# Gate and up projections of four SwiGLU layers by quadrants: seven block products in place of eight, with operand sums made on the chip

## The chip, the cores and the metric

The kernel runs on one core of a Trainium2 chip. TensorE (PE) multiplies, VectorE (DVE), ScalarE (ACT) and GpSimd (POOL) do elementwise work, and SyncE (SP) issues most DMAs. The metric is the device time of one execution in microseconds (us), the median of several runs.

## The reference, cut to what matters

A streaming encoder step over 560 columns (512 frames of a new stream, 32 of a running one, 16 meta tokens), two layers. Each layer is FFN, mixer, FFN: the first mixer is gated linear attention (GLA), the second multi-head latent attention (MLA). So there are four FFNs, called (1,0), (2,0), (1,1), (2,1): first or second FFN of layer 0 or 1. They run in this order: (1,0), GLA, (2,0), (1,1), MLA, (2,1). Each is

```python
def swiglu_half(h, norm_w, w_gate, w_up, w_down):   # h [560, 1024], D_FF = 2816
    hn = rmsnorm(h, norm_w)
    return h + 0.5 * ((jax.nn.silu(hn @ w_gate) * (hn @ w_up)) @ w_down)
```

All is float32.

## The kernel before, in words

Features lie on partitions, so `h` is 8 tiles of [128, 560]. The 560 columns are treated as two halves of 280 (272 in the last FFN, called hf 0 and hf 1), since a product goes to one PSUM bank.

Every operand of a matmul is split in two parts, `hi` (rounded to the fp32r type) and `lo` (the rest), and a product is three matmuls: hi·hi, lo·hi, hi·lo. `split` makes the parts with one ACT copy (L160, to `hi`) and one DVE subtraction (L161, to `lo`). A weight piece is [128, 1024] at most: a DMA to `raw` (2 buffers), then the split to `whi` and `wlo` (4 buffers each). `mm` (L188, L189, L191) sums over the tiles k of the contraction:

```python
for k, (xh, xl) in enumerate(xs):
    pe.matmul(out, hi[:, b0 + k, :], xh[:, c], start=k == 0, stop=False)      # L188
    pe.matmul(out, lo[:, b0 + k, :], xh[:, c], start=False, stop=False)       # L189
for k, (xh, xl) in enumerate(xs):
    pe.matmul(out, hi[:, b0 + k, :], xl[:, c], start=False, stop=k == n - 1)  # L191
```

`ffn` goes through the 22 tiles f of D_FF in three groups of 8, 7 and 7. For each f and each half it makes G (gate) and U (up), each with 24 matmuls over the 8 tiles of `h` (so 96 for one f). Then follow on DVE and ACT: `sg` = G times the norm's column scale `yn` (L279), Silu (ACT, L280), times the scale again (L281), `av` = U times `sg` (L283), and the split of `av` into `ah` and `al`. After a group its down projection runs: for 8 tiles m and two halves, 8 or 7 tiles of `ah`, `al`, three matmuls each, and DVE adds the result to `h` (L298). PSUM has 3 banks under the tag `ps` and 5 under `s`.

During the last group's down projection `after(m, hf)` is called for every updated piece of `h`: it makes the next stage's operand (`Normed.parts`: one ACT op L112, one DVE op L113) and the sum of squares for the norm (ACT L209, DVE L210). The norm's column scale is applied to results, so products needn't wait for it.

Tile's scheduler fixes at build time in which order each engine takes its instructions; the engines are in order and wait on semaphores. All pools of `ffn` are opened at its start and closed at its end. The start is written out by hand (`manual_schedule`): a first `h` piece of 280 KB, then the first weight in four pieces.

Of the kernel before, what the change touches and what calls it, by code (L numbers as in the profile page):

```python
# [18 lines left out]
P = 128  # L19
D = 1024  # L20
# [9 lines left out]
GROUPS = ((0, 8), (8, 15), (15, 22))  # L30
# [22 lines left out]
def weight_plan():  # L53
    """Offset and columns of every weight piece [128, columns]; plan lists (key, columns / 128) in the order of use."""
# [79 lines left out]

class Net:
    def __init__(self, ctx, tc, a):
        self.tc, self.nc, self.a, self.ctx = tc, tc.nc, a, ctx
        E = lambda **k: ctx.enter_context(tc.tile_pool(**k))
        self.g = E(name="g", bufs=1)
        self.w = E(name="w", bufs=4)  # L140
        self.xp = E(name="xp", bufs=20)
# [39 lines left out]
    def mm(self, out, w, b0, xs, cols):  # L181
        """out += sum over k of w[:, b0+k].T @ xs[k][:, cols], both operands in two parts."""
# [3 lines left out]
        pe = self.nc.tensor  # L186
        for k, (xh, xl) in enumerate(xs):
            pe.matmul(out, hi[:, b0 + k, :], xh[:, c], start=k == 0, stop=False)  # L188
            pe.matmul(out, lo[:, b0 + k, :], xh[:, c], start=False, stop=False)  # L189
        for k, (xh, xl) in enumerate(xs):  # L190
            pe.matmul(out, hi[:, b0 + k, :], xl[:, c], start=False, stop=k == n - 1)  # L191
# [20 lines left out]
    def rsqrt_mean(self, half, y, n, dim):  # L212
        """y[:, t] = 1 / sqrt(mean of squares of column t + eps), the same on every partition."""
# [41 lines left out]
    def ffn(self, i, l, xs, halves, after):  # L255
        nc = self.nc
        with self.tc.tile_pool(name=f"act{i}{l}", bufs=1) as ap, \
                self.tc.tile_pool(name=f"tmp{i}{l}", bufs=3) as tp:
            for gi, (f0, f1) in enumerate(GROUPS):
                acts = [(ap.tile([P, T], F32R, name=f"ah{j}", tag=f"ah{j}"),  # L260
                         ap.tile([P, T], F32R, name=f"al{j}", tag=f"al{j}")) for j in range(f1 - f0)]
                order = [(f, hf) for f in range(f0, f1) for hf in (0, 1)]
                if gi == 0:
                    order = [(f0, 0), (f0 + 1, 0), (f0, 1), (f0 + 1, 1)] + order[4:]
                L = {}
                for f, hf in order:
# [12 lines left out]
                    nc.vector.tensor_tensor(sg[:, :n], G[:, :n], y, op=ALU.mult)  # L279
                    nc.scalar.activation(sg[:, :n], sg[:, :n], AF.Silu)  # L280
                    nc.vector.tensor_tensor(sg[:, :n], sg[:, :n], y, op=ALU.mult)  # L281
                    av = tp.tile([P, 280], F32, name="av", tag="av")
                    nc.vector.tensor_tensor(av[:, :n], U[:, :n], sg[:, :n], op=ALU.mult)  # L283
                    self.split(acts[f - f0][0][:, c], acts[f - f0][1][:, c], av[:, :n])
                last = gi == len(GROUPS) - 1
                order = [(m, hf) for m in range(ND) for hf in (0, 1)]
                if last:
                    order = order[:8] + [(m, 0) for m in range(4, 8)] + [(m, 1) for m in range(4, 8)]
                L = {}
                for m, hf in order:  # L290
                    if m not in L:
                        L[m] = self.load(("d", i, l, gi, m))
                    c0, c1 = halves[hf]
                    n = c1 - c0
                    c = slice(c0, c1)
                    Y = self.bank()
                    self.mm(Y[:, :n], L[m], 0, acts, halves[hf])
                    nc.vector.scalar_tensor_tensor(self.h[:, m, c], Y[:, :n], 0.5, self.h[:, m, c],  # L298
                                                   op0=ALU.mult, op1=ALU.add)
# [23 lines left out]
    def gla(self, xs, after, one, con):  # L323
        nc, tc, a = self.nc, self.tc, self.a
        nv = self.nv
        mask, causal, causs, wgu, aTs, aTq, facs, onec = con
        bg, hn = NORM_COLS["bg"], NORM_COLS["hn"]
        with ExitStack() as es:
            E = lambda **k: es.enter_context(tc.tile_pool(**k))
            one = E(name="gl1b", bufs=1)  # L330
            two = E(name="gl2", bufs=2)
            op = E(name="glo", bufs=8)
# [3 lines left out]
            # the last 48 frames as one operand: the high parts in columns 0..47, the low parts in columns 64..111  # L336
# [26 lines left out]
            def values(h):  # L363
                """v of the head by frames; for the first head also the gate's low rank part."""
# [97 lines left out]
            for h in range(GH):  # L462
# [25 lines left out]
                # chunks: the group's 16 first frames, the running stream's frames, then pairs of 64  # L488
# [62 lines left out]
                # output gate, and the projections that fill the gaps of the chunks  # L551
# [43 lines left out]
            wout(1)  # L595

# [14 lines left out]
    def softmax(self, pool, p, parts):  # L611
        """p = softmax over the columns of all parts (tile, rows' column count, first column in p)."""
# [16 lines left out]
    def mla_constants(self, one):  # L629
# [12 lines left out]
        with self.tc.tile_pool(name="mlc", bufs=1) as tp:  # L642
# [15 lines left out]
    def mla(self, xs, after, one, kp, rp, ks, rs, kt, cq):  # L658
        nc, tc, a = self.nc, self.tc, self.a
        nv = self.nv  # L660
        (kph, kpl), (rph, rpl), (ksh, ksl), (rsh, rsl), (kth, ktl), (cqh, cql) = kp, rp, ks, rs, kt, cq
        with ExitStack() as es:
            E = lambda **k: es.enter_context(tc.tile_pool(**k))
            two = E(name="ml2", bufs=2)
            with tc.tile_pool(name="mlk", bufs=1) as kp:
# [79 lines left out]
                self.split(kth[:LS, 2, :], ktl[:LS, 2, :], tr[:LS, :256])  # L745
            cqs = [(cqh[:, m, :], cql[:, m, :]) for m in range(3)]
            self.attention(es, two, cqs, yq, [partial(f, 1) for f in (query_roots, query_norm)], kph, kpl, rph, rpl, ksh, ksl, rsh, rsl, kth, ktl, after)

    def attention(self, es, two, cqs, yq, query_norm, kph, kpl, rph, rpl, ksh, ksl, rsh, rsl, kth, ktl, after):
        nc, tc, a = self.nc, self.tc, self.a  # L750
        pe = nc.tensor
        E = lambda **k: es.enter_context(tc.tile_pool(**k))
        at = E(name="at", bufs=1)
# [41 lines left out]
        def sample(g):  # L795
            """The running stream's 32 frames of four heads, as 128 queries of the latent keys."""
# [19 lines left out]
            def latent2():  # L816
                """Every head's queries times the keys of all four; a head keeps its own."""
# [100 lines left out]
        def scores(h, t):  # L918
            """Softmax of the scores of 128 frames to pt[t]."""
# [54 lines left out]
        def wout(heads):  # L974
# [263 lines left out]
```

## Time and profile before

| what | us |
|---|---|
| median of 3 runs | 2156.37 (2156.29 to 2158.45) |
| span of the profiled execution | 2155.1 |
| PE busy | 2131.7 (16262 matmuls) |
| DVE busy | 1166.9 |
| ACT busy | 765.0 |
| POOL busy | 48.3 |

The profiled execution has no time of its own beside its span; the median lies 1.3 us above the span, which stands for what lies around it. Busy time counts overlapping matmuls once. The granted TensorE clock is 0.996 of full speed over the span.

### The profile page before, as it was taken

What the parts mean: (1) busy time and instruction counts of PE and PEld (TensorE: products, weight loads), DVE (VectorE), ACT (ScalarE), POOL (GpSimd) and SP (SyncE); (2) the same over time, 40 slices, a digit from 0 to 9 for tenths busy, and PEclk for the clock granted to TensorE, in tenths of its full rate; (3) what the DMA queues carried; (4) which work ended last, traced back from release to release, by engine and by line L of the source; (5) the groups of instructions that cost most, each with busy time, mean ns of one, the idle gap of its engine ahead of it and who ended that gap; (6) DMA issues with size and microseconds to landing.
All of it is one profiled execution on the core that took longest, in us unless ns stands there. A gap on an engine that the chain in (4) does not pass through costs nothing.

```text
span 2155.1 us, 38573 instructions
## 1 busy us (share of the span) xinstructions
PE 2131.7 (99%) x16262; PEld 2092.7 (97%) x16262; DVE 1166.9 (54%) x2487; ACT 765.0 (35%) x1463; POOL 48.3 (2%) x117
## 2 busy tenths in 40 slices
PE   8999999999999999999999999999999999999998
PEld 8999999989999999999999999999988899999997
DVE  7434444666657544434564344446787774344445
ACT  6212222455445322222342222224575553222231
POOL 0000000001110000000000000000110000000000
PEclk9999999999999999999999999999999999999999
DMA  5222222322222322232232222222111222222222
GB/s 164 84 89 85 83 89 74 90 68 76 65 81 74 98 87 81 84 93 79 88 91 89 88 79 89 87 86 85 57 58 42 88 79 88 89 86 84 96 78 72
DMA packets 57325, 180.17 MB, mean 84 GB/s; under 512 B 6384, under 2 KB 13936, under 8 KB 57152
## 3 DMA queue, kind: packets, MB, share of 16 engines
q1 hardware_dynamic: 53328, 173.07, 25.9%
q10 hardware_dynamic: 3824, 4.63, 0.7%
q8 instruction: 128, 2.10, 0.4%
q14 instruction: 45, 0.37, 0.1%
HBM read 173.69 MB, written 3.99 MB: 82 GB/s over the span
## 4 chain that ended last, share of the span: by engine, by line
PE 96%; DVE 2%; ACT 1%; DMA 1%; issue 0%; POOL 0%; SPq 0%; DVEq 0%; ACTq 0%; POOLq 0%
PE ps L188 21%; PE ps L191 20%; PE ps L189 20%; PE s L188 8%; PE s L191 8%; PE s L189 8%; PE ps L384 1%; PE ps L385 1%; PE ps L387 1%; PE ps L195 1%; PE s L195 1%; PE s L932 0%; PE s L948 0%; PE ps L196 0%; PE ps L197 0%
## 5 line engine op out<-in xcount | busy, mean ns | idle before, releaser
L160 ACT CAST whi<-raw 128x1024 fp32r<-128x1024 f32 (+4 forms) x351 | 342.9, 980 | 726.5 <-PE ps L191 555.8
L161 DVE TENSOR_TENSOR wlo<-raw,whi 128x1024 fp32r<-128x1024 f32 (+4 forms) x351 | 403.1, 1151 | 204.4 <-ACT whi L160 203.8
L188 PE MATMUL ps<-x,whi 128*128 128x280 f32 (+1 forms) x1872 | 497.4, 295 | 8.9 <-ACT whi L160 6.2
L189 PE MATMUL ps<-x,wlo 128*128 128x280 f32 (+1 forms) x1872 | 491.7, 292 | 0.0
L188 PE MATMUL s<-x,whi 128*128 128x280 f32 (+1 forms) x1424 | 371.3, 291 | 0.0
L189 PE MATMUL s<-x,wlo 128*128 128x280 f32 (+1 forms) x1424 | 370.4, 290 | 0.0
L188 PE MATMUL ps<-ah,whi 128*128 128x280 f32 (+1 forms) x1408 | 368.3, 290 | 0.0
L189 PE MATMUL ps<-ah,wlo 128*128 128x280 f32 (+1 forms) x1408 | 368.3, 291 | 0.0
L188 PEld LDWEIGHTS ps<-x,whi 128*128 128x128 f32 x1872 | 353.8, 189 | 13.6 <-ACT whi L160 6.2
L189 PEld LDWEIGHTS ps<-x,wlo 128*128 128x128 f32 x1872 | 353.9, 189 | 0.8 <-DVE wlo L161 0.2
L191 PE MATMUL ps<-x,whi 128*128 128x280 f32 (+1 forms) x1872 | 285.1, 291 | 0.0
L188 PEld LDWEIGHTS s<-x,whi 128*128 128x128 f32 x1424 | 268.2, 188 | 0.1
L189 PEld LDWEIGHTS s<-x,wlo 128*128 128x128 f32 x1424 | 267.7, 188 | 0.1
L188 PEld LDWEIGHTS ps<-ah,whi 128*128 128x128 f32 x1408 | 264.8, 188 | 0.0
L189 PEld LDWEIGHTS ps<-ah,wlo 128*128 128x128 f32 x1408 | 264.8, 188 | 0.0
L191 PEld LDWEIGHTS ps<-x,whi 128*128 128x128 f32 x1872 | 256.5, 189 | 0.5
L191 PE MATMUL ps<-al,whi 128*128 128x280 f32 (+1 forms) x1408 | 211.6, 291 | 0.0
L191 PE MATMUL s<-x,whi 128*128 128x280 f32 (+1 forms) x1424 | 211.2, 290 | 0.0
L298 DVE SCALAR_TENSOR_TENSOR h<-ps,h 128x280 f32<-128x280 f32 (+1 forms) x192 | 85.9, 447 | 227.2 <-PE ps L191 227.0
L191 PEld LDWEIGHTS s<-x,whi 128*128 128x128 f32 x1424 | 192.6, 188 | 0.0
L191 PEld LDWEIGHTS ps<-al,whi 128*128 128x128 f32 x1408 | 192.2, 188 | 0.0
L279 DVE TENSOR_TENSOR sg<-ps,yn 128x280 f32<-128x280 f32 (+1 forms) x176 | 78.0, 447 | 166.0 <-PE ps L191 165.6
(323 smaller groups left out, 2084.5 us busy)
## 6 DMA issues: line engine op xcount, KB each, us to landing
raw<-W SPq DMA_DIRECT2D x256, 512.0 KB, 3.5
raw<-W SPq DMA_DIRECT2D x64, 448.0 KB, 3.3
raw<-W SPq DMA_DIRECT2D x4, 384.0 KB, 3.1
h<-xT SPq DMA_DIRECT2D x2, 560.0 KB, 6.1
o_y<-h SPq DMA_DIRECT2D x8, 136.0 KB, 1.8
o_y<-h ACTq DMA_DIRECT2D x8, 136.0 KB, 1.8
raw<-W SPq DMA_DIRECT2D x8, 128.0 KB, 2.1
raw<-W SPq DMA_DIRECT2D x4, 256.0 KB, 2.7
```

Of the source, the lines that this page charges most:

```text
L160: self.nc.scalar.copy(hi, src)
L161: self.nc.vector.tensor_tensor(lo, src, hi.bitcast(F32), op=ALU.subtract)
L188: pe.matmul(out, hi[:, b0 + k, :], xh[:, c], start=k == 0, stop=False)
L189: pe.matmul(out, lo[:, b0 + k, :], xh[:, c], start=False, stop=False)
L191: pe.matmul(out, hi[:, b0 + k, :], xl[:, c], start=False, stop=k == n - 1)
L195: pe.matmul(out, a[0], b[0], start=first, stop=False)
L279: nc.vector.tensor_tensor(sg[:, :n], G[:, :n], y, op=ALU.mult)
L298: nc.vector.scalar_tensor_tensor(self.h[:, m, c], Y[:, :n], 0.5, self.h[:, m, c], op0=ALU.mult, op1=ALU.add)
L384: nc.tensor.matmul(out, xh[:, c0:c1], wh, start=wh is ks[0][0], stop=False)
L385: nc.tensor.matmul(out, xl[:, c0:c1], wh, start=False, stop=False)
L387: nc.tensor.matmul(out, xh[:, c0:c1], wl, start=False, stop=wl is ks[-1][1])
```

## The change

**Seven products for eight.** Two tiles f are taken as a pair. The pair's weights (gate, or up) are a 2 by 2 block matrix: rows f and f+1, columns the first four and last four tiles of `h`. The operand is one too: first and last four tiles of `h`, half 0 and half 1. Gate and up of the pair took 8 block products each way (192 matmuls with both); by the Strassen-Winograd scheme they take 7 (168). The price is sums: of weight blocks, of operand blocks, and of results.

- `quads`: the four blocks of gate and up together, [128, 1024] each, come by 8 DMAs of 256 KB into the pool `raw` (tiles `fr`, 7 buffers). POOL makes four sums of [128, 1024] in float32 (L345 of the changed kernel). Seven blocks are split instead of four pieces (L235 on ACT, L236 on DVE).
- `Quads.parts`, in place of `Normed.parts` ahead of an FFN: seven operands of 4 tiles instead of the two halves as they are. Per FFN it is 36 ACT and 44 DVE ops of 280 columns in place of 16 and 16.
- `gate_up`: results are summed by 8 ACT copies from PSUM to SBUF and 8 DVE ops that add a copy to a bank (L407, L428). A and C share products, so banks live longer: A is two `ps` banks, B, C, D two `s` banks each.
- Groups of 6, 6, 6 and 4 tiles in place of 8, 7, 7: four down projections per FFN, each with 16 updates of `h`.
- Pools are opened and closed by stage (`Pools`), on the left and right side of SBUF in turn, so that a stage's memory is used again by the next. The constants of GLA and MLA are loaded at their mixer's start.
- The hand-written start is gone: four pieces of `h` of 560 KB, all operands, then weights, in the scheduler's order.

```diff
-GROUPS = ((0, 8), (8, 15), (15, 22))
+GROUPS = ((0, 6), (6, 12), (12, 18), (18, 22))
...
+class Quads(Normed):
+    OPS = ("b11", "b21", "b22", "t5", "t6", "t4", "t7")
...
+        if hf == 0:
+            self.made("b11" if m < 4 else "b21", i, h=piece(m, 0), w=weight(m))
+        elif m < 4:
+            b12, t5 = self.temp("b12", 4), self.temp("t5", 4)
+            nc.scalar.activation(b12, piece(m, 1), AF.Copy, scale=weight(m))
+            v.scalar_tensor_tensor(t5, piece(m, 0), weight(m), b12, op0=ALU.mult, op1=ALU.subtract)
+            self.made("t5", i, src=t5)
+            self.kept[i] = b12, t5
+        else:
+            b12, t5 = self.kept.pop(i)
+            b22, t6, t4, t7 = (self.temp(x, 2) for x in ("b22", "t6", "t4", "t7"))
+            nc.scalar.activation(b22, piece(m, 1), AF.Copy, scale=weight(m))
+            v.scalar_tensor_tensor(t6, t5, -1.0, b22, op0=ALU.mult, op1=ALU.subtract)
+            self.made("t6", i, src=t6)
+            self.made("b22", i, src=b22)
+            v.tensor_tensor(t7, b22, b12, op=ALU.subtract)
+            self.made("t7", i, src=t7)
+            v.scalar_tensor_tensor(t4, piece(m, 0), weight(m), t6, op0=ALU.mult, op1=ALU.add)
+            self.made("t4", i, src=t4)
...
+    def quads(self, i, l, f, raws):
...
+        r11, r12, r21, r22 = raw
+        s1, s2 = (raws.tile([P, 8 * P], F32, name="fr", tag="fr") for _ in range(2))
+        add = lambda out, x, y: nc.gpsimd.tensor_tensor(out, x, y, op=ALU.add)
...
+        yield parts(r11)
+        yield parts(r12)
+        add(s1, r21, r22)
+        add(s2, s1, r11)
+        yield parts(s2)
+        yield parts(s1)
+        add(r21, r21, r11)
+        yield parts(r21)
+        yield parts(r22)
+        add(r12, r12, s2)
+        yield parts(r12)
...
+        fresh(A, "ps")
+        product(A, "b11")
+        r1 = copies(A)
+        fresh(C, "s")
+        product(C, "b21")
+        add(C, r1)
+        finish(0, 0, *C, 1)
+        product(A, "t6", True)
+        r2 = copies(A)
+        fresh(B, "s")
+        product(B, "t5")
+        p5 = copies(B)
+        product(A, "t7", True)
+        r3 = copies(A)
+        add(A, p5)
+        finish(1, 1, *A, -1)
+        fresh(D, "s")
+        product(D, "t4")
+        for t, x in zip(D, r3):
+            v.tensor_tensor(t[:, :n], x[:, :n], t[:, :n], op=ALU.subtract)
+        finish(1, 0, *D, -1)
+        product(B, "b22", True)
+        add(B, r2)
+        finish(0, 1, *B, 1)
...
-                    self.mm(G[:, :n], wg, 0, xs, halves[hf])
-                    self.mm(U[:, :n], wu, 0, xs, halves[hf])
...
+            for f in range(f0, f1, 2):
+                self.gate_up(i, l, f, xs, acts[f - f0:f - f0 + 2], raws, tp)
...
             if last:
+                fw.close()
+                after = turn()
```

`product` is 24 matmuls, a gate and an up block with 12 each; `finish` is the chain of L279 to L283 and the split of `av`, as before, for one half of one f. In what follows the products of a pair are numbered in the order in which the kernel takes them, 1 (`b11`) to 7 (`b22`).

How the order of the instructions changes is shown at three places. The first is DVE in the middle of a group, where gate and up run; `wlo` is a weight's low part, `sg`, `av`, `al` are as above, `r` a copy of a bank, `ps` and `s` are PSUM banks. Before:

```order
L279 TENSOR_TENSOR sg_1839<-ps_1789,yn_96 128x280
L281 TENSOR_TENSOR sg_1839<-sg_1839,yn_96 128x280
L283 TENSOR_TENSOR av_1843<-s_1790,sg_1839 128x280
L161 TENSOR_TENSOR al0_1764<-av_1843,ah0_1763 128x280
L279 TENSOR_TENSOR sg_1897<-ps_1847,yn_96 128x280
L161 TENSOR_TENSOR wlo_2035<-raw_2033,whi_2034 128x1024
```

And now, up to the split for product 3 of the next pair (from the sum of product 6 of the pair that is being finished):

```order
L428 TENSOR_TENSOR s_2006<-r_1992,s_2006 128x280
L401 SCALAR_TENSOR_TENSOR av_1999<-ps_1808,sg_1998 128x280
L428 TENSOR_TENSOR s_2007<-r_1994,s_2007 128x280
L395 SCALAR_TENSOR_TENSOR sg_2038<-s_2006,yn_111 128x280
L236 TENSOR_TENSOR al3_1524<-av_1999,ah3_1523 128x280
L407 TENSOR_TENSOR s_1929<-s_1929,r_1925 128x280
L397 TENSOR_TENSOR sg_2038<-sg_2038,yn_111 128x280
L393 TENSOR_TENSOR sg_2077<-s_1929,yn_111 128x280
L401 SCALAR_TENSOR_TENSOR av_2039<-s_2007,sg_2038 128x280
L407 TENSOR_TENSOR s_1930<-s_1930,r_1927 128x280
L397 TENSOR_TENSOR sg_2077<-sg_2077,yn_111 128x280
L236 TENSOR_TENSOR wlo_2176<-fr_2100,whi_2175 128x1024
```

DVE now sums banks between the scalings, and its next weight split stands behind sums that wait for the pair's last products. The second place is POOL, which had nothing to do in an FFN and now has four sums a pair, here of two pairs (the tiles are s1, r21, s2, r12 of each):

```order
L345 TENSOR_TENSOR fr_1821<-fr_1815,fr_1818 128x1024
L345 TENSOR_TENSOR fr_1815<-fr_1815,fr_1809 128x1024
L345 TENSOR_TENSOR fr_1822<-fr_1821,fr_1809 128x1024
L345 TENSOR_TENSOR fr_1812<-fr_1812,fr_1822 128x1024
L345 TENSOR_TENSOR fr_2099<-fr_2093,fr_2096 128x1024
L345 TENSOR_TENSOR fr_2093<-fr_2093,fr_2087 128x1024
```

The sums of a pair stand one behind the other, and the last two rows' pair needs buffers that the pair ahead frees. The third place is DVE at the border from FFN (2,0) to (1,1), where the last piece of `h` becomes an operand (`x`, `t4` to `t7`, `b22` are operands, `acc` is the sum of squares, `ps_11974` and `ps_12877` are the last down product). Before:

```order
L298 SCALAR_TENSOR_TENSOR h_70<-ps_11946,h_70 128x280
L161 TENSOR_TENSOR wlo_12152<-raw_12150,whi_12151 128x1024
L113 SCALAR_TENSOR_TENSOR x_11533<-h_70,nv_71,x_11532 128x280
L210 TENSOR_TENSOR acc_11566<-acc_11566,sq_11971 128x280
L298 SCALAR_TENSOR_TENSOR h_70<-ps_11974,h_70 128x280
```

And now, for the last piece, up to the weight split for product 3 of the next FFN:

```order
L191 TENSOR_TENSOR t7_12894<-b22_12891,b12_12669 128x280
L193 SCALAR_TENSOR_TENSOR t4_12893<-h_67,nv_68,t6_12892 128x280
L236 TENSOR_TENSOR x_12498<-t6_12892,x_12498 128x280
L236 TENSOR_TENSOR x_12490<-b22_12891,x_12490 128x280
L236 TENSOR_TENSOR x_12506<-t7_12894,x_12506 128x280
L236 TENSOR_TENSOR x_12502<-t4_12893,x_12502 128x280
L286 TENSOR_TENSOR acc_12532<-acc_12532,sq_12907 128x280
L320 TENSOR_SCALAR vh_13015<-s_13013 128x280
L407 TENSOR_TENSOR s_12981<-s_12981,r_12977 128x280
L407 TENSOR_TENSOR s_12982<-s_12982,r_12979 128x280
L321 TENSOR_SCALAR yn_12507<-vh_13015 128x280
L236 TENSOR_TENSOR wlo_13039<-fr_12948,whi_13038 128x1024
```

One operand op for a piece has become seven, and the split for product 3 stands behind those of all pieces: 41 rows lie between the update of the piece (m 4, hf 1) of `h` and this split.

More of the change, by code (lines that the diff above doesn't have):

```diff
@@ L185, in mm @@
         n = len(xs)
-        pe = self.nc.tensor
+        f = partial(self.nc.tensor.matmul, out, skip_group_check=more)
         for k, (xh, xl) in enumerate(xs):
-            pe.matmul(out, hi[:, b0 + k, :], xh[:, c], start=k == 0, stop=False)
-            pe.matmul(out, lo[:, b0 + k, :], xh[:, c], start=False, stop=False)
+            f(hi[:, b0 + k, :], xh[:, c], start=not more and k == 0, stop=False)
+            f(lo[:, b0 + k, :], xh[:, c], start=False, stop=False)
         for k, (xh, xl) in enumerate(xs):
-            pe.matmul(out, hi[:, b0 + k, :], xl[:, c], start=False, stop=k == n - 1)
+            f(hi[:, b0 + k, :], xl[:, c], start=False, stop=k == n - 1)
     def mm3(self, out, a, b, first, last):
@@ new lines, in quads @@
+        raw = []
+        for q in range(4):
+            t = raws.tile([P, 8 * P], F32, name="fr", tag="fr")
+            for j, x in enumerate("gu"):
+                off, n = PLAN[x, i, l, f + q // 2]
+                src = self.a["W"][off:off + P * n].rearrange("(p k c) -> p k c", p=P, k=2)[:, q % 2]
+                nc.sync.dma_start(t[:, 512 * j:512 * j + 512], src)
+            raw.append(t)
+        r11, r12, r21, r22 = raw
+        s1, s2 = (raws.tile([P, 8 * P], F32, name="fr", tag="fr") for _ in range(2))
@@ new lines, in quads, with parts @@
+        add = lambda out, x, y: nc.gpsimd.tensor_tensor(out, x, y, op=ALU.add)
+        def parts(src):
+            hi = self.w.tile([P, 8, P], F32R, name="whi", tag="whi")
+            lo = self.w.tile([P, 8, P], F32R, name="wlo", tag="wlo")
+            self.split(*(t.rearrange("p a b -> p (a b)") for t in (hi, lo)), src)
+            return hi, lo
+        yield parts(r11)
[4 more added lines that the diff above has]
+        yield parts(s1)
@@ new lines, in quads, with gate_up, product, copies @@
+        add(r21, r21, r11)
[3 more added lines that the diff above has]
+        yield parts(r12)
+    def gate_up(self, i, l, f, xs, act, raws, tp):
+        nc = self.nc
+        v = nc.vector
+        n = xs.n
+        left = self.quads(i, l, f, raws)
+        A, B, C, D = [], [], [], []
+        fresh = lambda to, tag: to.extend(self.bank(tag) for _ in range(2))
+        def product(to, op, more=False):
+            w, x = next(left), xs.operand(op)
+            for j in range(2):
+                self.mm(to[j][:, :n], w, 4 * j, x, (0, n), more)
+        def copies(of):
+            out = []
+            for t in of:
+                r = tp.tile([P, 280], F32, name="r", tag="r", bufs=8)
+                nc.scalar.copy(r[:, :n], t[:, :n])
+                out.append(r)
+            return out
+        def finish(j, hf, G, U, sign):
+            y = xs.scale(hf)
+            sg = tp.tile([P, 280], F32, name="sg", tag="sg", bufs=3)[:, :n]
+            av = tp.tile([P, 280], F32, name="av", tag="av", bufs=3)[:, :n]
+            g, u = G[:, :n], U[:, :n]
+            if sign > 0:
+                v.tensor_tensor(sg, g, y, op=ALU.mult)
+            else:
+                v.scalar_tensor_tensor(sg, g, -1.0, y, op0=ALU.mult, op1=ALU.mult)
+            nc.scalar.activation(sg, sg, AF.Silu)
+            v.tensor_tensor(sg, sg, y, op=ALU.mult)
+            if sign > 0:
+                v.tensor_tensor(av, u, sg, op=ALU.mult)
+            else:
+                v.scalar_tensor_tensor(av, u, -1.0, sg, op0=ALU.mult, op1=ALU.mult)
+            c = slice(*xs.halves[hf])
+            self.split(act[j][0][:, c], act[j][1][:, c], av)
+        def add(banks, r):
+            for t, x in zip(banks, r):
+                v.tensor_tensor(t[:, :n], t[:, :n], x[:, :n], op=ALU.add)
+        fresh(A, "ps")
[22 more added lines that the diff above has]
+        finish(0, 1, *B, 1)
@@ new lines, in ffn @@
+    def ffn(self, i, l, xs, halves, side, turn):
+        nc = self.nc
+        ap, fw = Pools(self.tc, side), Pools(self.tc, side)
+        acp = ap(f"act{i}{l}")
+        raws, tp = fw(f"raw{i}{l}", 7), fw(f"tmp{i}{l}", 1)
+        after = None
+        for gi, (f0, f1) in enumerate(GROUPS):
+            last = gi == len(GROUPS) - 1
+            acts = [(acp.tile([P, T], F32R, name=f"ah{j}", tag=f"ah{j}"),
+                     acp.tile([P, T], F32R, name=f"al{j}", tag=f"al{j}")) for j in range(f1 - f0)]
+            for f in range(f0, f1, 2):
+                self.gate_up(i, l, f, xs, acts[f - f0:f - f0 + 2], raws, tp)
+            order = [(m, hf) for m in range(ND) for hf in (0, 1)]
+            if last:
+                fw.close()
+                after = turn()
+                order = order[:8] + [(m, 0) for m in range(4, 8)] + [(m, 1) for m in range(4, 8)]
+            L = {}
+            for m, hf in order:
+                if m not in L:
+                    L[m] = self.load(("d", i, l, gi, m))
+                c0, c1 = halves[hf]
+                n = c1 - c0
+                c = slice(c0, c1)
+                Y = self.bank()
+                self.mm(Y[:, :n], L[m], 0, acts, halves[hf])
+                nc.vector.scalar_tensor_tensor(self.h[:, m, c], Y[:, :n], 0.5, self.h[:, m, c],
+                                               op0=ALU.mult, op1=ALU.add)
+                if last:
+                    after(m, hf)
+        ap.close()
```

213 lines of the change are left out of this document (115 added, 98 removed).

## The prediction

> **What bounds the kernel now.** I read the busy times and the chain of the page first, then TensorE's waits, then the matmul rate by stretches.
>
> ```profile
> span 2155.1 us, 38573 instructions
> PE 2131.7 (99%) x16262; PEld 2092.7 (97%) x16262; DVE 1166.9 (54%) x2487; ACT 765.0 (35%) x1463; POOL 48.3 (2%) x117
> PE 96%; DVE 2%; ACT 1%; DMA 1%; issue 0%; POOL 0%; SPq 0%; DVEq 0%; ACTq 0%; POOLq 0%
> PE ps L188 <- ACT whi L160: 6.2, 1, 6.2
> PE s L237 <- DVE ry L252: 2.2, 1, 2.2
> ...
> PE ps L188 <- DVE sg L279: 0.2, 1, 0.2
> 0.00:50.00 50.00, 41.74 (x299) 40.83 (x299) 38.70 (x87) 32.55 (x70) 0.95 (x12) 1.00 0.50 163
> 50.00:400.00 350.00, 350.00 (x2710) 350.00 (x2709) 157.03 (x263) 93.82 (x150) 0.00 (x0) 1.00 0.28 86
> 1100.00:1480.00 380.00, 380.00 (x2946) 379.81 (x2945) 178.18 (x305) 105.36 (x169) 0.00 (x0) 1.00 0.28 85
> ```
>
> TensorE is never idle but for the start: the longest wait is the first weight, the rest is a few microseconds, and at the border of two FFNs (inside 1100 to 1480) there is none. In the stretch from 50 to 400 us (columns: length, busy time and instructions of PE, weight load, DVE, ACT, POOL, clock, DMA) 2710 matmuls take 350.00 us, 129.15 ns each. So fewer matmuls shorten the kernel one for one, as long as TensorE stays fed. In the first 50 us it does 299 matmuls, worth 38.6 us: the start loses 11.4 us.
>
> **The matmuls removed.** A pair of f had 192 matmuls, now 168; 11 pairs in each of 4 FFNs: 44 x 24 = 1056 fewer, times 129.15 ns = 136.4 us. The down projections keep their count. A pair's floor on TensorE goes from 24.8 to 168 x 0.12915 = 21.7 us.
>
> **What DVE must do for a pair.**
>
> ```profile
> L161 DVE TENSOR_TENSOR wlo<-raw,whi 128x1024 fp32r<-128x1024 f32 x252 | 312.7, 1242 | 165.8 <-ACT whi L160 165.4 <-PE ps L387 0.2
> L160 ACT CAST whi<-raw 128x1024 fp32r<-128x1024 f32 x252 | 264.2, 1049 | 555.4 <-PE ps L191 424.9 <-issue 108.4 <-PE s L191 12.8
> L298 DVE SCALAR_TENSOR_TENSOR h<-ps,h 128x280 f32<-128x280 f32 x144 | 64.7, 449 | 168.8 <-PE ps L191 168.8
> L283 DVE TENSOR_TENSOR av<-s,sg 128x280 f32<-128x280 f32 x132 | 58.8, 449 | 124.1 <-PE s L191 124.1
> L281 DVE TENSOR_TENSOR sg<-sg,yn 128x280 f32<-128x280 f32 x132 | 58.6, 447 | 29.1 <-ACT sg L280 28.7
> L280 ACT ACTIVATE sg<-sg 128x280 f32<-128x280 f32 x132 | 56.7, 434 | 129.9 <-DVE sg L279 129.9
> L160 ACT CAST ah<-av 128x280 fp32r<-128x280 f32 x132 | 55.6, 424 | 162.6 <-DVE av L283 162.6
> 199.51 1.23 DVE L161 TENSOR_TENSOR wlo<-raw,whi 128x1024 fp32r<-128x1024 f32 x1 [0.68 <-ACT whi L160]
> 200.66 0.44 DVE L161 TENSOR_TENSOR al<-av,ah 128x280 fp32r<-128x280 f32 x1
> 455.70 0.45 DVE L477 TENSOR_TENSOR kd<-kg,E 128x280 f32<-128x280 f32 x1
> 456.19 0.45 DVE L478 TENSOR_TENSOR kg<-kg,mn 128x280 f32<-128x280 f32 x1
> 456.56 0.44 DVE L422 SCALAR_TENSOR_TENSOR kg<-ps,yn 128x280 f32<-128x280 f32 x1
> ```
>
> A weight split lasts 1242 ns and the next op starts 1.15 us after it; ops of 280 columns last 0.45 us and follow each other at 0.37 us, or 0.49 where one uses the other's result. I take 0.40. Before, a pair was 4 splits and 16 ops, 4 x 1.15 + 16 x 0.40 = 11.0 of 24.8 us. Now it is 7 splits, the same 16 ops and 8 bank sums (priced as L283, also one bank and one SBUF tile): 7 x 1.15 + 24 x 0.40 = 17.7 of 21.7 us. ACT has 7 x 1.05 for `whi`, 8 x 0.43 for Silu and `ah`, 8 copies of a bank (the nearest row is the cast, 0.42): 14.2 us, so it does not bound.
>
> **What POOL does to DVE.**
>
> ```profile
> L608 POOL TENSOR_TENSOR sq<-sq,sin 128x272 f32<-128x272 f32 x8 | 6.2, 776 | 79.5 <-ACT sq L606 76.7 <-issue 2.7
> L484 POOL TENSOR_TENSOR qS<-qg,fac 128x512 f32<-128x512 f32 x4 | 4.2, 1040 | 0.0
> L458 POOL TENSOR_TENSOR elab<-E 128x4 f32<-128x4 f32 x4 | 0.8, 201 | 0.0
> 457.70 1.24 POOL L484 TENSOR_TENSOR kS<-kd,fac 128x512 f32<-128x512 f32 x1 [3.79 <-DVE kd L477]
> 457.96 2.06 DVE L161 TENSOR_TENSOR wlo<-raw,whi 128x1024 fp32r<-128x1024 f32 x1
> 1553.45 0.78 POOL L608 TENSOR_TENSOR sq<-sq,sin 128x272 f32<-128x272 f32 x1 [5.83 <-ACT sq L606]
> 1553.75 0.43 DVE L788 TENSOR_TENSOR vh<-ps,yn 128x272 f32<-128x272 f32 x1
> 1554.18 0.77 POOL L724 TENSOR_TENSOR cos<-cos,yn 128x272 f32<-128x272 f32 x1
> 1554.26 0.99 DVE L609 TENSOR_TENSOR y<-acc,sq 128x272 f32<-128x272 f32 x1
> ```
>
> The split that meets a POOL product takes 2.06 us instead of 1.23; `y`, with two inputs in SBUF, takes 0.99 instead of 0.44, while `vh`, which reads a PSUM bank, is not slowed. So while POOL runs a two-input op, DVE's ops on two SBUF tiles stand still, up to POOL's end. [...] In the sum by the trace it is a hold of so many us a pair:
>
> A sum of 1024 columns: from 201 ns for 4 and 776 for 272 columns, 2.15 ns a column, 2.39 us. Bounds: twice the 512 row, 2.08, and 776 in proportion, 2.92. Four are 9.6 us a pair. DVE escapes where its next ops read a bank (16 of 31, in runs of one to four, some 0.8 us for each sum): held 4 x 1.6 = 6.4 us. Together 17.7 + 6.4 = 24.1, say 24.0 with what falls into waits. So in a running group DVE, not TensorE, sets the pair, 2.3 above the floor. The bounds: no hold that counts (DVE has 4.0 us to spare), 0; all held, 27.3, 5.6 above.
>
> The first pair of a group is better off, since four splits and most sums were made during the down projection, where DVE has 16 x 0.45 and 8 smaller splits in 37 us: 0.5 above the floor. A FFN: 4 x 0.5 + 7 x 2.3 = 18; four: **+72**.
>
> **Group ends.** Each FFN has four instead of three. After product 7 the last half needs two bank sums, L279, Silu, L281, L283 and the cast, 2.6 us, and the order puts a down weight's split and other rows between, 1.7 us more. The first down product (18 matmuls, 2.3 us) covers part; its own input comes from product 6 by the same chain. Before, only L283 and cast followed the last matmul, and no wait shows. I take 2.5 us for 16 ends, **+40** (bounds 1 and 5 with DVE already late). The 64 added updates of `h` at 0.45 lie beside 37 us of matmuls and cost nothing there.
>
> **FFN entries.** From the update of piece (m 4, hf 1) TensorE has three down products of 12 matmuls and products 1 and 2: 84 x 0.129 = 10.8 us. DVE has 41 rows, two splits among them, and then the split for product 3: 3 x 1.15 + 39 x 0.42 = 19.8, and 3.2 for two sums: 23.0. So product 3 waits 12 us, and DVE trails in the first pair, where the scale is also made: 5 more. Three entries of 17: **+51** (bounds 5 and 25 each; after a mixer three of the four blocks' buffers also lie where the last operands were, so their DMAs, 3.5 us in the middle, start at the mixer's end). Constants of the mixers, loaded later, have 20 us and more before use: 0, up to 3 each.
>
> **The start.**
>
> ```profile
> raw<-W SPq DMA_DIRECT2D x256, 512.0 KB, 3.5
> h<-xT SPq DMA_DIRECT2D x2, 560.0 KB, 6.1
> 6.18 0.60 PE L188 MATMUL ps<-x,whi 128*128 128x280 f32 x1 [6.18 <-ACT whi L160]
> ```
>
> TensorE began at 6.2 us. Now the first piece of `h` is 560 KB (5 to 6 us), and DVE's split for product 1 stands behind 43 operand ops, 18 us, which all use two SBUF tiles and meet three sums, 7 us: product 1 at about 31 us. Less the 11.4 lost before, +20, and 4 for the first pair's trail: **+24** (10 to 35).
>
> **Sum.** -136.4 + 72 + 40 + 51 + 24 = +51 on the 2155.1 of the span; with the 1.3 between span and median, 2207 us.
>
> **Rivals.**
> - *TensorE stays the bound in gate and up.* POOL's sums fall into DVE's waits for the banks (up to 4.0 us a pair are free, a hold of 1.0 per sum). For it: before, DVE is idle between nearly all ops of a pair. Against: the order has splits and SBUF scalings among the sums. Pairs +10, ends +25, entries +45, start +24: -136 + 104 = -32, 2124. It decides from a hold under 4.0 us.
> - *TensorE decides alone.* It is 99% busy; DVE's 1167 with 3 x 44 splits (164) and 8 x 44 sums (158) and operands (50) is 1540, 72%. Then all but start and half the entries is hidden: 2156 - 136 + 24 + 20 = 2064. [...] Against it: DVE is 81% full within a pair without any hold.
> - *DVE is held nearly throughout.* 8.8 of 9.6 us count: 26.5 a pair, +142; ends 60, entries 60, start 28: 2156 - 136 + 290 = 2310.
> - *The buffers are the bound.* Seven for six a pair: s1 of the next pair waits for a DMA (3.5) that waits for this pair's last sum; four sums, the DMA, splits between and holds are 9.6 + 3.5 + 4 x 2.5 = 23 a pair. Near the forecast, 2215.
>
> **Chances.** The forecast 0.43 (its own range 2165 to 2250), TensorE stays the bound 0.24, TensorE alone 0.05, held throughout 0.12, buffers 0.10, and 0.06 for a balance within 0.2% (4 us, what a measurement can tell from no change). Faster 0.29, same 0.06, slower 0.65. The range leaves out the lone TensorE and part of the held case: 2115 to 2290.
>
> **What would show it.** Right: TensorE waits in the gate and up stretches for `wlo` (L236) and bank sums; pairs of about 24 us; POOL near 420 us busy or more; `wlo` of 1024 columns well over 1.24 us on the mean; gaps of some 12 us at product 3 of three FFNs; first steady matmuls near 31 us. Wrong: pairs at 21.7, `wlo` still near 1.3, or POOL's sum far from 2.4 us. The forecast fails most easily at the hold, which 28 of 44 pairs multiply, and at how far DVE runs ahead at group ends.

## The result and the profile after

The changed kernel takes 2261.1 us (median of 4 runs, 2258.39 to 2266.71), the kernel before 2156.64: the ratio is 1.0484, with a 95% interval of 1.0469 to 1.0499. The profiled execution has a span of 2260.2, 105.1 more than before; the forecast was +51. First the page's span, busy times and chain, then TensorE's longest waits (total, times, longest):

```profile
span 2260.2 us, 38422 instructions
PE 2060.9 (91%) x15206; PEld 2003.4 (89%) x15206; DVE 1740.3 (77%) x3171; ACT 1030.1 (46%) x2050; POOL 535.9 (24%) x293
PE 59%; DVE 28%; issue 5%; ACT 5%; DMA 3%; POOL 1%; DVEq 0%; SPq 0%; ACTq 0%; POOLq 0%
```

```profile
PE ps L264 <- ACT ah L235: 78.0, 13, 6.7
PE ps L264 <- ACT whi L235: 34.4, 3, 26.3
PE ps L264 <- ACT r L383: 18.2, 11, 5.5
PE s L265 <- DVE wlo L236: 9.2, 7, 7.2
```

TensorE lost the 1056 matmuls as forecast (16262 - 15206), but it is now idle for 9% of the span, and DVE holds 28% of the chain. One wait stands out: 13 times TensorE waits for `ah`, up to 6.7 us. In 12 of these 13 it is the first down product of a group that waits for the last f's input. The groups by line show what was priced, POOL's sum and DVE's splits (busy, mean ns of one):

```profile
L345 POOL TENSOR_TENSOR fr<-fr 128x1024 f32<-128x1024 f32 x176 | 487.0, 2777 | 1249.7 <-issue 569.7 <-DMA fr<-W 444.6 <-ACT r L383 42.9
L236 DVE TENSOR_TENSOR wlo<-fr,whi 128x1024 fp32r<-128x1024 f32 x308 | 482.6, 1572 | 72.8 <-ACT whi L235 72.6
L236 DVE TENSOR_TENSOR al<-av,ah 128x280 fp32r<-128x280 f32 x132 | 107.7, 817 | 22.1 <-ACT ah L235 21.1
```

A sum on POOL takes 2.78 us (forecast 2.39, 2.08 to 2.92), a weight split 1572 ns instead of 1242, the split of `av` 817 where an op of this size takes 447. Last, one group of FFN (1,0) by stretches: its three pairs and its down projection (length, then busy time and instructions of PE, weight load, DVE, ACT, POOL; clock; DMA).

```profile
159.25:180.87 21.62, 21.62 (x170) 21.62 (x169) 17.69 (x22) 11.52 (x20) 10.13 (x4) 1.00 0.26 87
180.87:202.49 21.62, 21.62 (x171) 21.62 (x170) 20.56 (x27) 12.18 (x22) 9.68 (x4) 1.00 0.23 75
202.49:224.38 21.89, 21.89 (x170) 21.70 (x169) 21.36 (x28) 9.47 (x19) 10.72 (x4) 1.00 0.28 96
224.38:270.63 46.25, 39.66 (x291) 39.44 (x289) 23.58 (x43) 11.54 (x17) 2.40 (x1) 0.93 0.28 87
```

The pairs are at TensorE's floor of 21.7, not at 24. The loss lies behind them: 46.25 us for 288 matmuls worth 37.2. Yet DVE did not keep up in the pairs: it rested 1.1 and 0.5 us in the second and third, and shows 22, 27 and 28 ops where the run without POOL's sums, below, has 25, 32 and 34. It falls behind (it trails), and TensorE meets that only at the group's end, where a second thing comes on top. What happens there, first on DVE, then on POOL, then on TensorE:

```profile
214.60 0.45 DVE L399 TENSOR_TENSOR av<-s,sg 128x280 f32<-128x280 f32 x1
215.54 2.35 DVE L236 TENSOR_TENSOR al<-av,ah 128x280 fp32r<-128x280 f32 x1 [0.49 <-ACT ah L235]
217.81 3.42 DVE L236 TENSOR_TENSOR wlo<-fr,whi 128x1024 fp32r<-128x1024 f32 x1
221.15 3.14 DVE L236 TENSOR_TENSOR wlo<-raw,whi 128x768 fp32r<-128x768 f32 x1
224.22 0.45 DVE L407 TENSOR_TENSOR ps<-ps,r 128x280 f32<-128x280 f32 x1
```

```profile
215.17 8.31 POOL L345 TENSOR_TENSOR fr<-fr 128x1024 f32<-128x1024 f32 x3 [10.11 <-DVE av L399]
```

```profile
225.54 0.29 PE L265 MATMUL ps<-ah,wlo 128*128 128x280 f32 x1
232.42 0.60 PE L264 MATMUL ps<-ah,whi 128*128 128x280 f32 x1 [6.59 <-ACT ah L235]
232.82 0.43 PE L265 MATMUL ps<-ah,wlo 128*128 128x280 f32 x1
...
237.02 0.43 PE L265 MATMUL ps<-ah,wlo 128*128 128x280 f32 x1
```

POOL makes three sums in one burst of 8.31 us. They are for the first pair of the next group, whose product 3 begins some 61 us later (270.6 + 6.2). In each of the 12 groups that have a next one, such a burst begins 8.1 to 9.9 us before the group's first down matmul. Three DVE ops take 8.9 us in place of 2.6 meanwhile, and behind them stands the chain that ends in the last `ah`. TensorE runs dry 1.4 us into the down projection, waits 6.6, and then makes its matmuls at a distance of 0.23 us in place of 0.13 for nearly 5 us (clock 0.93 over the stretch).

Where the 105 us lie can be worked out from the starts of the matmuls: the length of each stretch, less its matmuls at the pace of before (0.1292 us, 0.1253 in the last FFN). "First group" runs from a FFN's first matmul to its first down product; an entry is that group with what the stretch ahead of the FFN grew. The other columns are experiments below.

| place, us | forecast | changed | late sums | tiny sums | sums on DVE |
|---|---|---|---|---|---|
| matmuls removed | -136 | -136 | -136 | -136 | -136 |
| pairs and group ends, without the first groups' pairs | 92 | 112 | 30 | 4 | 9 |
| three entries with first groups | 66 | 88 | 86 | 40 | 74 |
| start with first group, less 11.4 to 11.8 before | 29 | 37 | 35 | 17 | 26 |
| tail | 0 | 3 | 3 | 3 | 3 |
| span against before | +51 | +105 | +19 | -72 | -23 |

(The forecast's pairs, +72, are spread here: 5 for each of the four first groups. The parts meet the measured spans within 1 us. Of what the stretches ahead of the FFNs grew in the changed kernel, 4.4 us lie in the first half of GLA and 3.1 in that of MLA, away from the entry itself.)

### The profile page after: what moved, and what is told of

Its sections match the earlier page's. It is cut to its first block, busy times and chain, and to the rows that moved or that the text cites. A ratio compares the mean times of both kernels' runs of the same rounds, so it can differ in the third digit from the quotient of the medians.

```text
span 2260.2 us, 38422 instructions
## 1 busy us (share of the span) xinstructions
PE 2060.9 (91%) x15206; PEld 2003.4 (89%) x15206; DVE 1740.3 (77%) x3171; ACT 1030.1 (46%) x2050; POOL 535.9 (24%) x293
## 4 chain that ended last, share of the span: by engine, by line
PE 59%; DVE 28%; issue 5%; ACT 5%; DMA 3%; POOL 1%; DVEq 0%; SPq 0%; ACTq 0%; POOLq 0%
PE ps L264 14%; PE ps L267 14%; PE ps L265 13%; DVE wlo L236 12%; PE s L265 3%; PE s L267 3%; PE s L264 3%; ACT whi L235 2%; DMA raw<-W 2%; DVE sg L397 2%; DVE al L236 2%; DVE x L236 1%; DVE ps L407 1%; DVE s L407 1%; DVE yn L328 1%
## 5 line engine op out<-in xcount | busy, mean ns | idle before, releaser
L345 POOL TENSOR_TENSOR fr<-fr 128x1024 f32<-128x1024 f32 x176 | 487.0, 2777 | 1249.7 <-issue 569.7
L236 DVE TENSOR_TENSOR wlo<-fr,whi 128x1024 fp32r<-128x1024 f32 x308 | 482.6, 1572 | 72.8 <-ACT whi L235 72.6
L264 PE MATMUL ps<-x,whi 128*128 128x280 f32 (+1 forms) x1520 | 417.6, 300 | 61.1 <-ACT whi L235 34.4
L235 ACT CAST whi<-fr 128x1024 fp32r<-128x1024 f32 x308 | 321.1, 1049 | 218.2 <-PE ps L267 143.4
L265 PE MATMUL ps<-x,wlo 128*128 128x280 f32 (+1 forms) x1520 | 412.2, 297 | 7.8 <-DVE wlo L236 7.7
L264 PEld LDWEIGHTS ps<-x,whi 128*128 128x128 f32 x1520 | 292.1, 192 | 70.3 <-ACT whi L235 34.8
L265 PEld LDWEIGHTS ps<-x,wlo 128*128 128x128 f32 x1520 | 292.7, 193 | 11.7 <-DVE wlo L236 11.3
L264 PEld LDWEIGHTS s<-x,whi 128*128 128x128 f32 x1424 | 270.9, 191 | 23.0 <-DVE vh L320 9.4
L235 ACT CAST whi<-raw 128x768 fp32r<-128x768 f32 (+5 forms) x199 | 163.4, 823 | 240.6 <-PE ps L267 208.0
L236 DVE TENSOR_TENSOR wlo<-raw,whi 128x768 fp32r<-128x768 f32 (+5 forms) x199 | 219.6, 1105 | 64.9 <-ACT whi L235 64.3
L267 PE MATMUL ps<-x,whi 128*128 128x280 f32 (+1 forms) x1520 | 258.7, 295 | 0.0
L267 PEld LDWEIGHTS ps<-x,whi 128*128 128x128 f32 x1520 | 221.0, 192 | 0.6
```

The source lines that it names most:

```text
L235: self.nc.scalar.copy(hi, src)
L236: self.nc.vector.tensor_tensor(lo, src, hi.bitcast(F32), op=ALU.subtract)
L264: f(hi[:, b0 + k, :], xh[:, c], start=not more and k == 0, stop=False)
L265: f(lo[:, b0 + k, :], xh[:, c], start=False, stop=False)
L267: f(hi[:, b0 + k, :], xl[:, c], start=False, stop=k == n - 1)
L345: add = lambda out, x, y: nc.gpsimd.tensor_tensor(out, x, y, op=ALU.add)
```

## The experiments

Each is an edit to the changed kernel, run beside the kernel before; times are medians.

**1. The sums cut to 4 columns.** The kernel then leaves the weight sums out, so its result is not the layer's, and a pair takes four buffers in place of six.

```diff
-        add(s1, r21, r22)
-        add(s2, s1, r11)
-        yield parts(s2)
-        yield parts(s1)
+        add(r21, r22)          # add: out[:, :4] += x[:, :4]
+        add(r21, r11)
+        yield parts(r21)
+        yield parts(r21)
...
```

> The changed kernel with POOL's four sums of a pair cut to 4 columns each and made in place (so the products take unsummed blocks); order, splits, products, bank sums and groups stay. Theory A (held ends): three sums for the next group's first pair run in one burst of 8.3 us just when DVE makes the chain to `ah` of the group's last f, hold it for some 6.5 us, and TensorE then runs at half rate for 3 to 5 us; 12 of the 16 group ends cost 8.5 us each for that. Then the ends' waits fall under 1.5 us and, with the holds at the entries and the start gone as well (some 5 us each), the span is about 2260 - 102 - 20 = 2138 (2120 to 2155). Theory B (long chain): bank sums, Silu, scalings and the down split after the last product are what is late, with or without POOL; then the ends still wait 5 us or more and the span is above 2225.

Measured: 2086.9 us, 0.968 of before (0.966 to 0.970), 51 us below what theory A gave. The three pairs of a group, the down projection of the first group, and the weight split in this run:

```profile
132.10:153.72 21.62, 21.62 (x170) 21.62 (x169) 14.67 (x25) 11.64 (x20) 0.80 (x4) 1.00 0.29 99
153.72:175.33 21.61, 21.61 (x170) 21.61 (x169) 17.47 (x32) 12.82 (x23) 1.89 (x4) 1.00 0.29 99
175.33:196.95 21.62, 21.62 (x171) 21.62 (x170) 17.93 (x34) 12.38 (x23) 1.66 (x4) 1.00 0.42 135
94.71:132.10 37.39, 37.39 (x290) 37.12 (x289) 17.40 (x30) 8.40 (x11) 0.00 (x0) 1.00 0.21 64
L236 DVE TENSOR_TENSOR wlo<-fr,whi 128x1024 fp32r<-128x1024 f32 x308 | 376.8, 1224 | 137.1 <-ACT whi L235 133.6 <-PE s L267 2.4 <-DMA fr<-W 0.5
```

The down projection needs 37.39 us with TensorE busy throughout: the chain behind the last product costs nothing by itself. Theory B falls. POOL's sums as a whole (the hold, their own time and the buffers that they need, which this run does not tell apart) cost 177 us of span (2260.2 against 2082.7): by the table 108 at the group ends, 48 at the entries, 20 at the start. The split is back at 1224 ns, and DVE's work for a pair without a hold is 17.5 to 17.9 us (second and third).

**2. The next group's sums made later.**

```diff
+        if late:               # first pair of groups 2 to 4
+            nc.gpsimd.tensor_copy(s1[:, :1], self.h[:, 1, :1])
         add(s1, r21, r22)
```

> The changed kernel with one instruction more on POOL: ahead of the sums of the first pair of the second, third and fourth group it copies one column of h's tile 1 after that tile's update in the down projection before, so these sums (nothing is left out) start some 6 us after the group's last product instead of beside it. A (held ends): the 12 waits of about 6.8 us at the first down product fall under 1.5 us, the half-rate stretches behind them vanish, about 2260 - 100 = 2160 (2145 to 2175); the sums then lie in the down projection, where DVE has slack. B (long chain): no change beyond 10 us, 2250 to 2262.

Measured: 2174.8 us (2171.59 to 2176.32), 1.0081 of before (1.0066 to 1.0096): 86 us less than the changed kernel, of the 100 expected. Its wait for `ah`, and POOL at the same group end:

```profile
PE ps L264 <- ACT ah L235: 16.1, 13, 1.8
227.13 0.18 POOL L356 COPY fr<-h 128x1 f32<-128x1 f32 x1 [28.49 <-DVE h L463]
227.40 7.84 POOL L345 TENSOR_TENSOR fr<-fr 128x1024 f32<-128x1024 f32 x3
```

The same three sums, for as long, now beside the down projection, cost little: 78.0 us of waits became 16.1. So it is when POOL runs, not that it runs, that costs the 12 ends. Left are 1.4 to 1.8 us an end in the first three FFNs (0.7 to 3.6 in the last) and about 1 us in each third pair.

**3. Another order of the last pieces of h** (with the late sums). The same is done in the mixers' last products, and `t4` is made when both halves of a piece are there.

```diff
-order = order[:8] + [(m, 0) for m in range(4, 8)] + [(m, 1) for m in range(4, 8)]
+order = order[:8] + [(m, 1) for m in range(4, 8)] + [(m, 0) for m in range(4, 8)]
...
```

> As with the late sums, and in the last down projection of a FFN (and of a mixer) the pieces (m 4 to 7, half 1) come ahead of (m 4 to 7, half 0), so that after the last piece of h two operand chains are left (b21 and t4, 4 DVE ops a piece with the split) in place of 6 or 7 ops. If the entries cost what DVE has queued behind the last pieces, each of the three entries (about 20 us over TensorE's floor in the first group) gets 6 to 10 us shorter: 2160 - 24 = 2136 (2128 to 2150). If the entry is set by something else (the four blocks' DMAs, or POOL's sums that hold DVE there), it stays within 5 us of the run with late sums alone.

Measured: 2176.1 us (2171.43 to 2185.11), the same as without it: a miss. The longest wait in the first products of FFN (1,1), first with the late sums alone, then here:

```profile
1120.93 0.90 PE L264 MATMUL ps<-x,whi 128*128 128x280 f32 x2 [5.50 <-ACT r L385]
```

```profile
1113.33 0.60 PE L269 MATMUL ps<-x,wlo 128*128 128x280 f32 x1 [4.37 <-DVE wlo L240]
```

The wait at product 3 is now one at product 1. The first groups of the later FFNs got 1.6 to 5.5 us shorter, and the stretches ahead of them 1.9 to 6.6 us longer: the wait only moves ahead. That fits a limit by the amount of DVE's work there, not by its order, but this run alone does not show it.

**4. The sums on DVE.**

```diff
-        add = lambda out, x, y: nc.gpsimd.tensor_tensor(out, x, y, op=ALU.add)
+        add = lambda out, x, y: nc.vector.tensor_tensor(out, x, y, op=ALU.add)
```

> The changed kernel with the four sums of a pair on DVE in place of POOL (nothing is left out). It takes the shared hold away and gives DVE 4 x 1.15 = 4.6 us more a pair: DVE was busy 20.6 of the 21.6 us of a steady pair, about 5 of them held, so it would be busy 20.2. A (held ends): pairs stay at 21.6, and the ends cost only what the scheduler puts there, 1 to 4 us each: 2165 to 2200. If a hold costs DVE less than the sum itself would (sums mostly beside ops that read banks), pairs now go over the floor by 1 to 3 us, and the time stays near 2260 or above. B (long chain): ends unchanged, 2250 or more.

Measured: 2133.6 us (2128.44 to 2136.17), 0.9889 of before (0.9874 to 0.9904), faster than expected, and 1.1% faster than the kernel before. The sum in its group, and a steady pair:

```profile
L345 DVE TENSOR_TENSOR fr<-fr 128x1024 f32<-128x1024 f32 x176 | 214.6, 1222 | 21.1 <-DMA fr<-W 19.4 <-DVE s L407 0.6 <-DVE sg L397 0.4
162.86:184.47 21.61, 21.61 (x170) 21.61 (x169) 21.06 (x36) 12.94 (x23) 0.00 (x0) 1.00 0.30 99
```

DVE makes a sum in 1.22 us. On POOL the sums lengthened DVE's ops by 273 us (each DVE op over the usual length of its kind, 286 us in all, less the 11 to 16 that kernels without these sums show), 1.55 us for each of 176. Handing the sum over cost DVE more than making it.

**5. The waits at the group ends filled with matmuls that nobody needs.**

```diff
                 Y = self.bank()
+                if (m, hf) == (0, 0) and not last:
+                    for _ in range(54):
+                        nc.tensor.matmul(Y[:, :xs.n], L[m][0][:, 0, :], xs.operand("b22")[0][0], start=True, stop=True)
```

> The changed kernel with 54 matmuls more ahead of the first down product of the first three groups of each FFN (648 in all); they write the bank that this product then starts afresh, so nothing else changes. 54 x 0.129 = 7.0 us fill the wait of about 6.8 us for the last `ah`, which DVE and ACT make as before. If TensorE runs at half rate behind such a wait because it stood idle (the trace shows a pitch of 0.235 in place of 0.117 to 0.129 us for 3 to 5 us after each), the 12 half-rate stretches vanish: 12 x about 1.9 = 23 us less, 2238 (2230 to 2248), with more matmuls than before. If the half rate has another cause, the filling only costs what it oversteps the wait: 2262 to 2285.

Measured: 2242.3 us (2237.89 to 2245.61), 19 less than the changed kernel with 648 matmuls more. TensorE's wait for `ah` and the stretch around the same group end:

```profile
PE ps L264 <- ACT ah L235: 1.5, 2, 0.9
220.00:234.00 14.00, 14.00 (x110) 13.89 (x109) 13.12 (x22) 4.68 (x10) 3.14 (x1) 1.00 0.41 128
```

In this stretch the filling matmuls stand where the wait was. DVE's chain is as late as before (the bank sum behind the burst starts at 223.88 us here and at 224.22 in the changed kernel, where the group ends 0.4 us later); the half rate behind the wait is gone: 110 matmuls in these 14.00 us, 0.127 us each, at a granted clock of 1.00, where the changed kernel has 19 in the 4.60 us behind its wait (232.42 to 237.02), 0.24 us each, at 0.50. Over the run the clock is 0.981 for 0.963. So it was the idle TensorE that brought it.

**6. The first weight blocks ahead of the operands** (with the sums on DVE; the splits of these blocks get the same priority).

```diff
+                with up() if q < 2 else nullcontext():      # up: high priority in the very first pair
                     nc.sync.dma_start(t[:, 512 * j:512 * j + 512], src)
...
```

> The sums on DVE as before, and at the very start the DMAs and splits of the first two weight blocks are put ahead of the operands (by the scheduler's priority); nothing is left out. The first matmul, at 19.7 us with the sums on DVE, then needs only one block and four operand tiles: about 9 to 10 us. If the start is set by when TensorE begins, all of these 10 us are gained: 2124. If it is set by DVE, which has 43 operand ops before product 3 can run whatever comes first, products 1 and 2 are done earlier and product 3 waits longer: within 3 us of 2133.

Measured: 2130.4 us (2126.88 to 2133.5), within 4 us of the run without it, as the second case had it:

```profile
9.78 0.60 PE L264 MATMUL ps<-x,whi 128*128 128x280 f32 x1 [9.78 <-ACT x L161]
32.56 0.83 PE L264 MATMUL ps<-x,whi 128*128 128x280 f32 x2 [14.56 <-ACT whi L235]
```

TensorE starts at 9.8 in place of 19.7 us and then waits 14.6 for a weight whose sum and split stand behind the operands on DVE. The start is DVE's.

**7. t5 second** (with the above; the sum s1 and its split move up with it).

```diff
         r1 = copies(A)
+        fresh(B, "s")
+        product(B, "t5")
+        p5 = copies(B)
         fresh(C, "s")
         product(C, "b21")
...
```

> As the one with the first blocks ahead, and in every pair the product with t5 comes second instead of fourth; nothing is left out. t5 needs only the first four tiles of h, which at an entry are ready long before the last pieces. So TensorE has 3 products instead of 2 (3.1 us more) before it needs DVE's last operand ops: if DVE's queue at the entry is the limit, each of three entries and the start gets about 3 us shorter, 12 us less than the one before. If TensorE at the entries waits for weights (blocks that come late, or the sum s1, now needed second), nothing is gained or up to 10 us lost.

Measured: 2116.0 us (2114.14 to 2125.14), 0.982 of before (0.979 to 0.985), 14 less than run 6. FFNs (2,0) and (1,1), from their first matmuls to their last, are 8.8 and 6.6 us shorter; the start gave none. This version is 1.8% faster than the kernel before.

**8. Two sums more a pair on POOL**, into a tile that nobody reads.

```diff
         yield parts(r12)
+        junk = raws.tile([P, 8 * P], F32, name="junk", tag="junk", bufs=1)
+        add(junk, r12, s2)
+        add(junk, r12, s2)
```

> The changed kernel with two sums more a pair on POOL into a tile that nobody reads, behind the fourth. Two theories on why its steady pairs stay at 21.6 us: (a) DVE is busy 20.6 of 21.6 us there, about 5 of them held, so a balance with 1 us to spare; two sums more hold it 2 to 4 us more, steady pairs go to 22.6 to 24.6 us (32 steady pairs: +30 to +95) and the ends get worse by up to 4 us each (+50): 2300 to 2400. (b) The sums fall mostly into DVE's waits and cost little wherever DVE isn't late already: steady pairs stay under 21.8, and only the ends get longer: 2260 to 2310.

Measured: 2371.2 us (2 runs), 1.0992 of before (1.0967 to 1.1016). The three pairs of a group:

```profile
170.60:192.21 21.61, 21.61 (x170) 21.61 (x169) 17.87 (x20) 10.86 (x19) 10.89 (x5) 1.00 0.27 95
192.21:215.71 23.50, 22.17 (x170) 21.73 (x169) 22.97 (x25) 10.83 (x21) 14.64 (x6) 1.00 0.21 72
215.71:245.16 29.45, 24.87 (x171) 24.27 (x169) 28.35 (x36) 12.36 (x24) 15.64 (x6) 0.88 0.25 81
```

Case (a), but not as a steady rate: the first pair is at the floor, the second 1.9, the third 7.8 us over it, with DVE resting 0.5 and 1.1 us in these two. DVE's trail grows from pair to pair, and with six sums TensorE meets it within the group.

**9. The first pair's sums and splits ahead of the operand ops** (with run 7's order; at the very start only the first block's DMAs now have priority).

```diff
-        up = self.tc.high_priority if first else nullcontext
+        up = self.tc.high_priority if f == 0 else nullcontext     # now around every sum and split of that pair
...
```

> As the one with t5 second, and the weight sums and splits of the first pair of each FFN are put ahead of the operand ops on DVE and ACT where both are ready (by the scheduler's priority); nothing is left out. With t5 second, TensorE still waits 10 us for a split at the third product of an FFN's first pair, since that split stands behind the operand ops of the last pieces of h, which only product 4 needs. If that order is what is left at the entries, these waits shrink by 5 us or more each and the start by some 8 us: 2090 to 2106. If DVE's amount of work there is the limit, product 4 then waits for its operand instead and the time stays at 2111 to 2120.

Measured: 2114.9 us (2112.45 to 2115.58), the same as run 7, as the second case had it. In the first pair of FFN (1,1) the third product that TensorE took needed 10.5 us in run 7 and 4.1 now (`b21` there, `b11` here), and the fourth, which needs the last operands, 3.2 and now 16.1. TensorE's wait there, ahead of the matmul that sums the squares for the norm:

```profile
1097.94 1.30 PE L292 MATMUL s<-acc,ones 128*128 128x280 f32 x2 [10.48 <-DVE acc L286]
```

## Why the prediction was right or wrong

The sign and the mechanism held: the sums on POOL hold DVE (its ops took 273 us longer with them), and what DVE cannot do in time eats more than the 136 us that the removed matmuls give. Without POOL's sums the change would gain 70 us (run 1). But the growth was twice the forecast: three steps failed, and the sizes of entries and start were too low.

**"In a running group DVE, not TensorE, sets the pair" was wrong, with both of its terms right.** DVE's work without a hold is 17.5 us a pair (17.7 forecast), the hold 273 / 44 = 6.2 on the mean of all pairs (6.4 forecast; 4.7 to 7.4 in the pairs of the second and third groups). Together 23.7 in a pair of 21.6 us, yet pairs took 21.6: the 32 pairs outside the first groups lost 8 us in all, where the forecast had 52. A rate that DVE cannot keep up with need not show at once: with six sums (run 8) a group's first pair was still at the floor, the second 1.9 and the third 7.8 us over it. In the changed kernel a group is three pairs, DVE enters it with a lead, and ends it with 77 ops done where run 1 has 91. The rival that TensorE stays the bound was right about the pairs, and wrong about the total.

**The group ends were taken as a chain of 2.5 us, for 16 ends alike.** The chain alone costs 0.2 to 0.5 (run 1: the first down product covers it). What costs is the trail and three sums for the next group that meet the chain: the down projections behind the 12 ends that have a next group in their FFN are 7.6 to 9.5 us too long, and 0.1 to 0.4 in three of the four that have none (the fourth, 5.2, is the border to FFN (1,1)). The prediction did not ask which sums POOL, with nothing else to do, would run at that moment. The burst is the greater part: run 2 moves it alone and takes 82 of the 108 us that run 1 takes, so some 26 are left for the trail. Pairs and ends together were forecast 92 (52 and 40) and measured 112 (8 and 104): the sums are near by luck, since the pairs' 52 stood in for what the ends lacked.

**No term for the clock behind a wait.** Matmuls that follow each other at 0.215 to 0.26 us cost 68 us over the usual 0.128 in the changed kernel, 27 before (nearly all in the mixers): some 40 us more, of the 54 that the sum lacks. The prediction read the granted clock as a column of its view only, and priced waits by their length alone. Run 5 shows the cause on 12 of the waits: 19 us back.

**Entries and start** were sized too low, 66 for 88 and 29 for 37. Their place fits (DVE behind the operand ops; runs 3, 6 and 9 only move the wait), but the hold there was put at 3.2 us an entry. At the border of (2,0) and (1,1) ops of DVE and TensorE read:

```profile
1157.94 2.65 DVE L193 SCALAR_TENSOR_TENSOR t<-h,nv,t 128x280 f32<-128x280 f32 x1
1167.49 0.89 PE L264 MATMUL ps<-x,whi 128*128 128x280 f32 x2 [5.50 <-ACT r L383]
1180.17 2.64 DVE L327 TENSOR_TENSOR t<-t,vh 128x280 f32<-128x280 f32 x1
1182.84 2.47 DVE L328 SCALAR_TENSOR_TENSOR yn<-t,yn 128x280 f32<-128x280 f32 x1
```

TensorE's row is its wait at product 3. Each of the three DVE ops, 0.4 to 0.5 us long elsewhere, waits out a sum and ends 0.3 us after it (the sums end at 1160.29, 1182.50 and 1185.00 us), two of them in the norm's scale, for which everything behind waits. Over their usual length DVE's ops took 10.5, 15.1 and 16.1 us more at the three entries (the first pair, and for (1,1) the down projection ahead of it). Run 1, with all that goes with the sums, takes 48 us off the entries, 16 each. At the start the first matmul came at 26.3 us and steady ones at 32 (31 forecast). But from 26.3 on the first pair lost 16 us, so that start and first pair together took 43 us off TensorE, where 31 and 4 were set aside.

The rest: the added `h` updates cost nothing, as forecast. That the constants cost nothing is not shown: the 4.4 and 3.1 us in the mixers' first halves, which the table counts among the entries, have a cause that stays open. The buffers as a bound would show in the steady pairs, which are at the floor. (That rival's 2215 does not follow from its 23 us a pair: in the prediction's own sum they give about 2180.) TensorE alone as the bound would have needed free sums; run 1 comes within 23 us of its 2064.

## What to carry to other kernels

Work that was handed to an idle engine was not free here: 1.55 us of DVE's time for a sum on POOL, where DVE makes it in 1.22. Ask what such work slows down, and when that engine will run it. Here 12 bursts of it, begun 8.1 to 9.9 us ahead of a group's first down matmul, met the one chain that TensorE waited for, and either a later start or the sums on DVE itself took most of the loss back. Where an engine needs more time per step than the step has, and the stretch is only a few steps long, work out how far it trails at the next hand-over rather than a longer step; and price a wait of TensorE of several us with its half-rate stretch behind it, here 1.1 to 2.4 us for a wait of 5.7 to 6.7.

## What the runs showed of the hardware

Between its first matmul and its tail TensorE had 18 idle stretches of 3.40 to 7.21 us in the changed kernel. Each was followed by 10 to 24 matmuls at double distance (0.215 to 0.26 us) among the next 29. Of the shorter ones, from 1 us up to the longest of 2.58, some were and some weren't: 14 such matmuls behind one of 1.62 us, one behind that of 2.58. Behind the waits at the group ends these stretches lasted 2.3 to 5.4 us and cost 1.1 to 2.4; run 5, which filled these waits, was 19 us shorter.

The ops of DVE that ran long in the group shown above ended behind a sum of POOL's: `al` of 0.44 us took 2.35 and ended at 217.89, 0.3 us after the burst's first sum (217.58); a split of 1.22 took 3.42 and ended at 221.23, 1.1 us after the second (220.14). POOL's sums varied too: one by itself took 2.40 us, as in the last stretch of the group shown above, and a quarter of all 176 took 3.26 or more.
